# A convolution stage that keeps its outputs in other pieces, loads its bands once and shifts its seven-product blocks by one

## The chip, the core and the metric

One core of one Trainium2 chip runs the whole program in one launch. The metric is device time in microseconds; the kernel before was run three times, and its median stands for it. The five instruction streams are TensorE (PE, with its weight loads PEld), VectorE (DVE), ScalarE (ACT), GpSimd (POOL) and SyncE (SP), which here issues every DMA, in order.

## The reference

A decoder trunk with two layers on x of 1024 tokens by 1024 channels, all in float32. Only layer 0's token mixer is touched by the change:

```python
def conformer_conv(x, w_in, b_in, w_dw, b_dw, ln_g, ln_b, w_out, b_out):
    h = x @ w_in + b_in                       # 1024 -> 2048 channels
    a, gate = jnp.split(h, 2, axis=-1)
    h = a * jax.nn.sigmoid(gate)
    h = lax.conv_general_dilated(             # causal, 31 taps, each channel by itself
        h, w_dw[:, None, :], window_strides=(1,), padding=[(CONV_WIDTH - 1, 0)],
        dimension_numbers=("NWC", "WIO", "NWC"), feature_group_count=D_MODEL) + b_dw
    h = jax.nn.silu(layer_norm(h, ln_g, ln_b))
    return h @ w_out + b_out
```

After it come, in layer 0, a residual layer norm, a squared-ReLU MLP of 4096 channels, a second layer norm and a gated embedding; in layer 1 the same with sliding-window attention as mixer. They hold most of the time and keep their code.

## The kernel before

**Exact products in three passes.** A float32 operand is split into a high part (a cast on ACT) and a low part (a subtraction on DVE), and each product is three matmuls: high by high, high by low, low by high (`mm3`). The names show it: xh and xl hold the transposed activations in quarters by channel half and token half, wh and wl a weight unit of 128 x 1024, raw its load.

**The order is written by a program.** Every operation is first recorded; `schedule()` then plays the list through with a price for each operation and a free time for each engine, takes the ready operation of least rank, and so fixes the order in which each engine gets its instructions. Tiles are slots of a named pool (X 8, A 9, B 8, E 4, z 4, t 5, g 4), given out in the order of the recorded list; an operation that needs one waits until a slot is free. `later(n)` pushes the rank back by n, `after(op)` adds a dependence. SP is one line: a DMA that waits holds up all behind it. In `schedule()` a DMA was priced by its bytes alone:

```python
            if e == "sync":
                v = o.allv[0]
                dma = max(dma, t + 1400.0) + v.n * v.parts / 75.0
                finish(o, max(dma, t + 2800.0))
```

**The convolution stage, `conv()`**, is two generators stepped in turn, `taps` six steps (LAG) behind `conv_in`, each with four steps for one of eight blocks c of 128 channels.

- `conv_in(c)` makes the gated input of block c. Blocks 0 to ALONE - 1 do it in full: two token halves by two channel sets (gate and a) by eight k blocks by three, 96 matmuls of 512 columns. The others go through `conv_seven`: seven products of half the size on each side instead of eight, 84 matmuls, from sums and differences of the weights (`pair_units`) and of the activations, the forms T1 to T4. `forms()` makes T1 to T3 from fresh loads of xT, ranked 200 later, into places borrowed from the pools A, bo, v, B and X; T4 overwrites the activations' own tiles (channels 0 to 511 of the second token half) when block ALONE begins (`last_forms`), and two more E tiles become bands.
- `hand_over` splits the result g into a tile zz (wh for the very last) and writes it in eight DMAs to the DRAM tiles scr, from where `taps` reads it into B as G in another arrangement.
- `taps(c)` runs the depthwise convolution on TensorE: for each half jj of a block two groups j, two matrices k each, nine shifts, 36 matmuls of 256 columns. The stationary operand is a band, a 128 x 1152 tile E whose 64 left columns hold the high part of the taps on all 128 partitions and whose right ones hold, on partitions 0 to 63 (HIGH), the low part. It is made from a load z of w_dw with 128 x 576 values, in which the host had written the same 64 rows twice. ACT copies z into E, DVE subtracts.
- The sums are biased, transposed back to tokens (tr) and, for c < KEPT, copied into a t tile and written to the DRAM tile kept. From block KEPT on they are copied straight into the tiles Z (eight from pool X, eight from A). When block KEPT begins, sixteen DMAs bring the kept blocks into Z; a token row there lies in pieces of 64 values, 256 B.
- `conv_ln` then normalises each token row of Z on DVE and POOL, transposes it and applies SiLU; `mix_out` multiplies with w_out. The projection of the embedding (`embed(0, ...)`) is ranked 300 later and fills in between; its results and the bands of the last blocks share the time with all of that.

The call of `embed`, `conv_ln` and `mix_out`, the MLPs and the attention are the same before and after.

Of the kernel before, what the change touches and what calls it, by code (L numbers as in the profile page):

```python
# [10 lines left out]
F32 = mybir.dt.float32  # L11
F32R = mybir.dt.float32r
# [3 lines left out]
P = 128  # L16
# [32 lines left out]
             ps=6, tr=2, sc=0, pv=0, mid=0)  # L49


ALONE = 3
KEPT = 7
FORMS_BY, BACK_BY = 200, 300
FORM_HOMES = ("A", 9), ("bo", 2), ("v", 1), ("B", 4), ("X", 8)
LATE = 100
# [66 lines left out]
class View:  # L123
# [30 lines left out]

    def to_broadcast(self, shape):
        return View(self.buf, np.broadcast_to(self.idx, shape[1:]), self.parts, self.steps + (("bro", shape),))

    def real(self):
        a = self.buf.tile
# [37 lines left out]
class Recorder:  # L197
# [120 lines left out]
    def schedule(self):  # L318
# [85 lines left out]
        while True:  # L404
            best = None
            for e in engs:
                while rdy[e] and rdy[e][0][2].end:
                    heapq.heappop(rdy[e])
                while fut[e] and fut[e][0][3].end:
                    heapq.heappop(fut[e])  # L410
                if rdy[e]:
                    t = free[e]
                elif fut[e]:
                    t = max(free[e], fut[e][0][0])
                else:
                    continue
                if best is None or t < best[0]:
                    best = (t, e)
            if best is None:
                break  # L420
            t, e = best
            while fut[e] and fut[e][0][0] <= t:
                r, p, i, o = heapq.heappop(fut[e])
                if not o.end:
                    heapq.heappush(rdy[e], (p, i, o))
            p, i, o = heapq.heappop(rdy[e])
            if WAIT and fut[e] and e != "tensor":
                r, p2, i2, o2 = fut[e][0]
                if not o2.end and r <= t + WAIT and p2 < p - 300:
                    heapq.heappush(rdy[e], (p, i, o))  # L430
                    heapq.heappop(fut[e])
                    t, o = r, o2
            if o.eng == "either":
                o.eng = e
                o.dur = self.cost(o, o.outv, o.allv)
            d = o.dur
            if e == "scalar" and o.name == "activation":
                k = TABLE.get(o.args[2].name if len(o.args) > 2 else "", 0)
                if k and k != table:
                    table = k  # L440
                    d += 1283.0
            if both(o):
                d += max(0.0, held["gpsimd" if e == "vector" else "vector"] - 50.0 - t)
                held[e] = t + d
            free[e] = t + d
            if e == "sync":
                v = o.allv[0]
                dma = max(dma, t + 1400.0) + v.n * v.parts / 75.0
                finish(o, max(dma, t + 2800.0))
            else:  # L450
                finish(o, t + d)
# [47 lines left out]
class Emit:  # L499
# [318 lines left out]
    def conv(self):  # L818
# [8 lines left out]
        ws.add(*[lambda k=k: self.prep(d["w_in"][0, k], range(4 * k, 4 * k + 4)) for k in range(2)])  # L827
        ws.pump()
        for c in range(1, 8):
            ws.add(*([d["w_in"][c, 0], d["w_in"][c, 1]] if c < ALONE else self.pair_units([d["w_in2"][c - ALONE, k] for k in range(2)])))  # L830
        nc.sync.dma_start(cc, d["cconst"])
        nc.sync.dma_start(self.ident, d["ident"])
        scr = {}
# [1 line left out]

        def hand_over(c, h, g):

            both = self.sb("wh" if (c, h) == (7, 0) else "zz", F32R, 2 * HT)
            self.split(g, both[:, 0:HT], both[:, HT : 2 * HT])
            for j in range(NG):  # L840
                if j % 2 == 0 and (c, j // 2) not in scr:
                    scr[c, j // 2] = nc.tile(f"scr{c}_{j // 2}", (P, 2 * U), F32, "DRAM")
                o = j % 2 * U + h * P
                cols = slice(o, o + P)
                dst = scr[c, j // 2].scatter(
                    lambda a, cols=cols: a.rearrange("(k p) u -> p k u", p=CG)[:, :, cols], CG, cols, 2 * PH
                )
                src = both.bitcast(F32)[j * CG : (j + 1) * CG, :].rearrange("p (k u) -> p k u", k=2 * PH)
                nc.sync.dma_start(dst, src)
# [84 lines left out]

        def conv_in(c):

            if c >= ALONE:
                yield from conv_seven(c)
                return
            us = ws.get(2)  # L940
            for h in (0, 1) if c == 0 else (1, 0):
                pp = [self.ps() for s in range(2)]

                def part(s, kb):
                    wh, wl = us[kb // 4]
                    o = (kb % 4) * 256 + (1 - s) * P
                    tr = [(wh[:, o : o + P], wl[:, o : o + P], *self.xs(kb, h * HT, HT))]
                    self.mm3(pp[s], tr, kb == 0, kb == KB - 1)

                if c == 0:  # L950
                    for kb in range(KB):
                        part(0, kb)
                        part(1, kb)
                    yield
                else:
                    for s in range(2):
                        for kb in range(KB):
                            part(s, kb)
                        if s == 0:
                            yield  # L960
                sg = self.sb("t")
                nc.scalar.activation(sg, pp[0], AF.Sigmoid, bias=bg[:, c : c + 1], scale=1.0)
                g = self.sb("t")
                nc.vector.scalar_tensor_tensor(
                    out=g, in0=pp[1], scalar=ba[:, c : c + 1], in1=sg, op0=ALU.add, op1=ALU.mult
                )
                hand_over(c, h, g)
                yield
            ws.done(2)
# [3 lines left out]
        def taps(c):  # L973
# [3 lines left out]
            for jj in range(2):  # L977
                pss = [self.ps() for k in range(2)]
                for j in range(2):
# [3 lines left out]
                    nc.sync.dma_start(G2[:, :, HIST : HIST + U], scr[c, 2 * jj + j].rearrange("p (k u) -> p k u", k=2))  # L983
                    exchange = nc.ops[-1]
                    for k in range(2):
                        w = nc.tile("z", (P, n))
                        nc.sync.dma_start(w, d["w_dw"][c, jj, 2 * j + k])
                        w = w.rearrange("p (m q) -> p m q", q=PH * CG)
                        e = bands[turn[0] % len(bands)]
                        turn[0] += 1  # L990
                        ev = e.rearrange("p (m o q) -> p m o q", o=2, q=PH * CG)
                        if e in fresh:
                            fresh.remove(e)
                            nc.gpsimd.memset(ev.bitcast(F32)[LOW, :, 1, :], 0.0)
                        nc.scalar.copy(ev[:, :, 0, :], w)
                        nc.vector.tensor_tensor(
                            out=ev[HIGH, :, 1, :], in0=w[HIGH], in1=ev[HIGH, :, 0, :].bitcast(F32), op=ALU.subtract
                        )
                        for i in range(SHIFTS):
                            o = k * LO + HIST - i  # L1000
                            nc.tensor.matmul(
                                pss[k][:, j * U : (j + 1) * U], e[:, i * P : (i + 1) * P], G[:, o : o + U],
                                start=i == 0, stop=i == SHIFTS - 1,
                            )
# [19 lines left out]
                        nc.tensor.transpose(pv[:, h, j], y[:, o : o + P], self.ident)  # L1024
                nc.slack = 0.0
                if c < KEPT:
                    s = self.sb("t")
                    (nc.scalar.copy if jj else nc.vector.tensor_copy)(s, pt)
                    nc.sync.dma_start(kept[:, (2 * c + jj) * HT : (2 * c + jj + 1) * HT], s)
                    yield  # L1030
                    continue
                if c == KEPT and jj == 0:
                    kv = kept.rearrange("p (c s u) -> p c s u", c=2 * KEPT, s=2 * PH)
                    for q in range(2):
                        m = min(8, 2 * KEPT - 8 * q)
                        for h in range(2):
                            for f in range(PH):
                                Z[h, f, q] = self.sb("XA"[q])
                                dst = Z[h, f, q][:, 0 : 64 * m].rearrange("p (c u) -> p c u", u=64)
                                with nc.later(BACK_BY):  # L1040
                                    nc.sync.dma_start(dst, kv[:, 8 * q : 8 * q + m, PH * h + f, :])
                for h in range(2):
                    for f in range(PH):
                        o = c % 4 * P + jj * 4 * CG
# [43 lines left out]
            forms()  # L1088
        more_bands()
        kept = self.dram("kept", 2 * KEPT * HT)  # L1090
        ins = (x for c in range(8) for x in conv_in(c))
        outs = (x for c in range(8) for x in taps(c))
        for n in range(32 + LAG):
# [902 lines left out]
def layout(a):  # L1996
# [12 lines left out]
    r["xT"] = c(x[phased].T.reshape(KB, P, T))  # L2009
    r["pT"] = c(np.stack([p[0][phased], p[1]]).transpose(0, 2, 1).reshape(2, 2, P, T))  # L2010
    wi = np.asarray(a["conv_w_in"])[0]
    r["w_in"] = c(wi.reshape(2, 4, P, 2, 8, P).transpose(4, 0, 2, 1, 3, 5).reshape(8, 2, P, 1024)[:ALONE])

    w2 = wi[:, np.concatenate([np.arange(D, 2 * D), np.arange(D)])].reshape(8, P, 2, 8, P)
    r["w_in2"] = c(w2.transpose(3, 2, 1, 0, 4).reshape(8, 2, P, 1024)[ALONE:])
# [12 lines left out]
    for q in range(CG):  # L2028
        band[:, :, :, :, q, :, q] = wt[:, :, :, :, q, :]
    band = band.reshape(8, 2, 4, P // 2, SHIFTS * PH * CG)  # L2030
    r["w_dw"] = c(np.concatenate([band, band], axis=3))

    bd = np.asarray(a["conv_b_dw"])[0].reshape(32, 2, CG).transpose(2, 1, 0).reshape(CG, 64)
    r["cconst"] = c(
# [45 lines left out]
```

## Time and profile before

| | us |
|---|---|
| runs | 2140.18, 2142.8, 2143.06 |
| median | 2142.8 |
| profiled execution | 2142.3 |
| its span, first to last instruction | 2140.5 |
| TensorE busy | 2116.5 |
| VectorE busy | 1757.5 |
| ScalarE busy | 1152.3 |
| GpSimd busy | 280.6 |

The mean granted TensorE clock is 0.999. The DMA moved 462.46 MB, of 228,939 packets 38,192 under 512 B. Nearly every instruction carries one line, L466, where the recorded list is issued, so rows are told apart by the tiles that they write and read: `ps<-xh,wl` is a matmul into PSUM, `E<-z` the making of a band, `X<-kept` a read of kept outputs. A group's mean for a matmul counts its pipelined duration (389 ns), which overlaps the next; how many of them start in a stretch says more. A row of a timeline gives start, duration, engine, line, operation, tiles and how many were merged.

### The profile page before, as it was taken

How to read it: one execution, taken by the hardware profiler on the slowest of the kernel's cores; microseconds unless marked ns; L12 is line 12 of the kernel's file. 1: busy time of each engine (PE TensorE's matmuls, PEld its weight loads, DVE VectorE, ACT ScalarE, POOL GpSimd, SP SyncE). 2: the span in 40 equal slices, each digit the busy share in tenths (PEclk: the TensorE clock that was granted, in tenths of full speed). 3: DMA queues.
4: the chain of work that ended last, by engine and by line, in shares of the span. 5: the costliest groups of instructions: out<-in, count | busy, mean ns of one | idle time of the engine just before them, and what ended most of it. 6: DMA issues, size and time to landing. Idle time of an engine off the chain costs nothing.

```text
span 2140.5 us, 29992 instructions
## 1 busy us (share of the span) xinstructions
PE 2116.5 (99%) x10008; PEld 1752.9 (82%) x10008; DVE 1757.5 (82%) x2854; ACT 1152.3 (54%) x2146; POOL 280.6 (13%) x495
## 2 busy tenths in 40 slices
PE   9999899999999999999999999999999999999999
PEld 7888778888888888888788888888888888888877
DVE  6866579988898788876986888689988988788688
ACT  5655554654544633335755888445445554333484
POOL 0000052200000000001320656240000000000042
PEclk9999999999999999999999999999999999999999
DMA  9877965867786756655487022665778795565726
GB/s 295 234 203 203 268 245 177 285 222 250 264 271 231 278 177 204 201 184 213 156 284 249 11 89 79 208 239 184 257 267 296 262 332 174 179 233 170 262 75 230
DMA packets 228939, 462.46 MB, mean 216 GB/s; under 512 B 38192, under 2 KB 64432, under 8 KB 228784
## 3 DMA queue, kind: packets, MB, share of 16 engines
q1 hardware_dynamic: 228784, 460.54, 65.1%
q8 instruction: 79, 1.29, 0.2%
q14 instruction: 76, 0.62, 0.1%
HBM read 312.34 MB, written 148.11 MB: 215 GB/s over the span
## 4 chain that ended last, share of the span: by engine, by line
PE 40%; DVE 5%; ACT 3%; DMA 2%; issue 1%; POOL 1%; SPq 0%; POOLq 0%; DVEq 0%; ACTq 0%
PE ps L466 31%; PE tr L466 9%; DVE xl L466 1%; DMA t<-proj 1%; ACT z L466 1%; DVE t L466 1%; POOL sm L466 1%; DVE z L466 1%; DVE sm L466 0%; DVE A L466 0%; DVE B L466 0%; ACT xh L466 0%; DMA raw<-in_w_kv_dram 0%; ACT t L466 0%; DMA raw<-gate_t 0%
## 5 line engine op out<-in xcount | busy, mean ns | idle before, releaser
L466 PE MATMUL ps<-xh,xl 128*128 128x512 f32 x636 | 247.6, 389 | 0.0
L466 PE MATMUL ps<-xh 128*128 128x512 f32 x636 | 247.6, 389 | 0.0
L466 PE MATMUL ps<-xl,xh 128*128 128x512 f32 x636 | 247.6, 389 | 0.0
L466 ACT CAST wh<-raw 128x1024 fp32r<-128x1024 f32 (+2 forms) x156 | 143.4, 923 | 134.7 <-PE ps L466 84.0
L466 POOL TENSOR_SCALAR sm<-sm 128x1 f32<-128x1 f32 x72 | 28.3, 397 | 1364.0 <-DVE E L466 612.0
L466 PE MATMUL ps<-xl,wh 128*128 128x512 f32 x508 | 198.7, 392 | 0.0
L466 PE MATMUL ps<-xh,wl 128*128 128x512 f32 x508 | 198.3, 391 | 0.0
L466 PE MATMUL ps<-xh,wh 128*128 128x512 f32 x508 | 196.1, 392 | 0.9 <-ACT xh L466 0.9
L466 PE MATMUL ps<-wh,xh 128*128 128x512 f32 (+1 forms) x404 | 159.2, 395 | 1.7 <-ACT zz L466 0.9
L466 PE MATMUL ps<-wh,xl 128*128 128x512 f32 (+1 forms) x404 | 160.4, 397 | 0.0
L466 PE MATMUL ps<-wl,xh 128*128 128x512 f32 (+1 forms) x404 | 159.3, 394 | 0.0
L466 ACT CAST wh<-g 128x512 fp32r<-128x512 f32 x128 | 76.4, 620 | 153.8 <-PE ps L466 73.7
L466 ACT CAST xh<-wh 128x1024 fp32r<-128x1024 f32 x76 | 79.7, 1049 | 118.0 <-PE tr L466 90.4
L466 PEld LDWEIGHTS ps<-xl,xh 128*128 128x128 f32 x636 | 119.4, 188 | 24.9
L466 PEld LDWEIGHTS ps<-xh,xl 128*128 128x128 f32 x636 | 119.4, 188 | 24.7
L466 PEld LDWEIGHTS ps<-xh 128*128 128x128 f32 x636 | 119.5, 188 | 24.6
L466 DVE TENSOR_TENSOR wl<-raw,wh 128x1024 fp32r<-128x1024 f32 (+1 forms) x100 | 100.0, 1001 | 35.5 <-ACT wh L466 35.1
L466 DVE TENSOR_TENSOR xl<-wh,xh 128x1024 fp32r<-128x1024 f32 x76 | 92.8, 1221 | 25.6 <-ACT xh L466 25.6
L466 PEld LDWEIGHTS ps<-xh,wh 128*128 128x128 f32 x508 | 95.4, 188 | 22.5 <-ACT xh L466 1.6
L466 PEld LDWEIGHTS ps<-xh,wl 128*128 128x128 f32 x508 | 95.5, 188 | 19.5
L466 PEld LDWEIGHTS ps<-xl,wh 128*128 128x128 f32 x508 | 95.4, 188 | 19.5 <-DVE xl L466 1.3
L466 DVE TENSOR_TENSOR wl<-g,wh 128x512 fp32r<-128x512 f32 x128 | 84.6, 686 | 26.8 <-ACT wh L466 26.8
(447 smaller groups left out, 5620.0 us busy)
## 6 DMA issues: line engine op xcount, KB each, us to landing
wh<-hid SPq DMA_DIRECT2D x78, 512.0 KB, 4.1
raw<-in_w_up_dram SPq DMA_DIRECT2D x61, 512.0 KB, 4.3
wl<-in_w_down_dram SPq DMA_DIRECT2D x58, 512.0 KB, 4.8
hid<-zz SPq DMA_DIRECT2D x96, 256.0 KB, 4.0
z<-in_w_dw_dram SPq DMA_DIRECT2D x64, 288.0 KB, 4.0
hid<-t SPq DMA_DIRECT2D x70, 256.0 KB, 3.0
raw<-hid SPq DMA_DIRECT2D x30, 512.0 KB, 3.7
B<-scr SPq DMA_DIRECT2D x32, 256.0 KB, 4.5
```

Of the source, the lines that this page charges most:

```text
L466: getattr(getattr(nc, o.eng), o.name)(*a, **k)
```

## The change

- `View.transfer()` is new: it counts the contiguous pieces of a view and prices 12 ns for each and 0.0476 ns for each byte, over 16. `schedule()` takes the larger of the two sides of a DMA instead of bytes over 75.
- ALONE 3 becomes 2, and block LAST = 7 is done in full: blocks 2 to 6 go by seven products. Because T4 has overwritten a quarter of the activations, `conv_in(7)` loads four blocks of xT again (`load_xT`), takes the token halves in the order 0, 1 and, in half 1, the blocks k from 4 on first. The very last `hand_over` is now (7, 1).
- KEPT 7 becomes 6. For the kept blocks the transposed result is copied by token half, h = 0 on DVE and h = 1 on ACT, into a t tile that holds both halves jj of the block, and written in one DMA for each h, in pieces of 128 values (512 B), to a layout in which each token phase has its six blocks side by side. The sixteen reads then take whole rows: 512 values for blocks 0 to 3, 256 for blocks 4 and 5.
- w_dw is stored once, 64 x 576. z has 64 partitions, ACT copies it twice (rows HIGH, rows LOW), DVE subtracts as before.

```diff
-ALONE = 3
-KEPT = 7
+ALONE = 2
+LAST = 7
+KEPT = 6
...
+    def transfer(self):
+        i = self.idx.ravel()
+        pieces = self.parts * (1 + int((np.diff(i) != 1).sum()))
+        return (12.0 * pieces + 0.0476 * 4 * i.size * self.parts) / 16
...
-                v = o.allv[0]
-                dma = max(dma, t + 1400.0) + v.n * v.parts / 75.0
+                dma = max(dma, t + 1400.0) + max(v.transfer() for v in o.allv)
...
-            if c >= ALONE:
+            if ALONE <= c < LAST:
                 yield from conv_seven(c)
                 return
             us = ws.get(2)
-            for h in (0, 1) if c == 0 else (1, 0):
+            if c == LAST:
+                for kb in range(KB // 2):
+                    self.load_xT(1, kb)
+            for h in (0, 1) if c in (0, LAST) else (1, 0):
                 pp = [self.ps() for s in range(2)]
+                order = [(kb + KB // 2 * (h if c == LAST else 0)) % KB for kb in range(KB)]
...
-                        w = nc.tile("z", (P, n))
+                        w = nc.tile("z", (P // 2, n))
...
-                        nc.scalar.copy(ev[:, :, 0, :], w)
+                        for rows in (HIGH, LOW):
+                            nc.scalar.copy(ev[rows, :, 0, :], w)
                         nc.vector.tensor_tensor(
-                            out=ev[HIGH, :, 1, :], in0=w[HIGH], in1=ev[HIGH, :, 0, :].bitcast(F32), op=ALU.subtract
+                            out=ev[HIGH, :, 1, :], in0=w, in1=ev[HIGH, :, 0, :].bitcast(F32), op=ALU.subtract
                         )
...
                 if c < KEPT:
-                    s = self.sb("t")
-                    (nc.scalar.copy if jj else nc.vector.tensor_copy)(s, pt)
-                    nc.sync.dma_start(kept[:, (2 * c + jj) * HT : (2 * c + jj + 1) * HT], s)
+                    for h in range(2):
+                        if jj == 0:
+                            wait[h] = self.sb("t")
+                        v = wait[h].rearrange("p (f j u) -> p f j u", f=PH, j=2)
+                        src = pt[:, h * 256 : (h + 1) * 256].rearrange("p (f u) -> p f u", f=PH)
+                        (nc.scalar.copy if h else nc.vector.tensor_copy)(v[:, :, jj, :], src)
+                        if jj:
+                            dst = kept.rearrange("p (s c u) -> p s c u", s=2 * PH, c=KEPT)
+                            nc.sync.dma_start(dst[:, PH * h : PH * h + PH, c, :], wait[h].rearrange("p (f u) -> p f u", f=PH))
...
-                                dst = Z[h, f, q][:, 0 : 64 * m].rearrange("p (c u) -> p c u", u=64)
+                                o = ((PH * h + f) * KEPT + 4 * q) * P
                                 with nc.later(BACK_BY):
-                                    nc.sync.dma_start(dst, kv[:, 8 * q : 8 * q + m, PH * h + f, :])
+                                    nc.sync.dma_start(Z[h, f, q][:, 0 : P * m], kept[:, o : o + P * m])
...
-    r["w_dw"] = c(np.concatenate([band, band], axis=3))
+    r["w_dw"] = c(band)
```

More of the change, by code (lines that the diff above doesn't have):

```diff
@@ L829, in conv @@
         for c in range(1, 8):
-            ws.add(*([d["w_in"][c, 0], d["w_in"][c, 1]] if c < ALONE else self.pair_units([d["w_in2"][c - ALONE, k] for k in range(2)])))
+            ws.add(*([d["w_in"][c, 0], d["w_in"][c, 1]] if c < ALONE or c >= LAST else self.pair_units([d["w_in2"][c - ALONE, k] for k in range(2)])))
         nc.sync.dma_start(cc, d["cconst"])
@@ L836, in hand_over @@
         def hand_over(c, h, g):
-            both = self.sb("wh" if (c, h) == (7, 0) else "zz", F32R, 2 * HT)
+            both = self.sb("wh" if (c, h) == (LAST, 1) else "zz", F32R, 2 * HT)
             self.split(g, both[:, 0:HT], both[:, HT : 2 * HT])
@@ L947, in part @@
                     tr = [(wh[:, o : o + P], wl[:, o : o + P], *self.xs(kb, h * HT, HT))]
-                    self.mm3(pp[s], tr, kb == 0, kb == KB - 1)
+                    self.mm3(pp[s], tr, kb == order[0], kb == order[-1])
                 if c == 0:
@@ L956, in conv_in @@
                     for s in range(2):
-                        for kb in range(KB):
+                        for kb in order:
                             part(s, kb)
@@ L1032, in taps @@
                 if c == KEPT and jj == 0:
-                    kv = kept.rearrange("p (c s u) -> p c s u", c=2 * KEPT, s=2 * PH)
                     for q in range(2):
-                        m = min(8, 2 * KEPT - 8 * q)
+                        m = min(4, KEPT - 4 * q)
                         for h in range(2):
@@ L1090, in conv @@
         kept = self.dram("kept", 2 * KEPT * HT)
+        wait = {}
         ins = (x for c in range(8) for x in conv_in(c))
@@ L2011, in layout @@
     wi = np.asarray(a["conv_w_in"])[0]
-    r["w_in"] = c(wi.reshape(2, 4, P, 2, 8, P).transpose(4, 0, 2, 1, 3, 5).reshape(8, 2, P, 1024)[:ALONE])
+    r["w_in"] = c(wi.reshape(2, 4, P, 2, 8, P).transpose(4, 0, 2, 1, 3, 5).reshape(8, 2, P, 1024))
     w2 = wi[:, np.concatenate([np.arange(D, 2 * D), np.arange(D)])].reshape(8, P, 2, 8, P)
```

## The prediction, made before the changed kernel was run

> **What bounds the kernel now.** I read the page first, then busy time by stretch, then the waits, and last the order of time around the one place that stands out.
>
> ```profile
> span 2140.5 us, 29992 instructions
> PE 2116.5 (99%) x10008; PEld 1752.9 (82%) x10008; DVE 1757.5 (82%) x2854; ACT 1152.3 (54%) x2146; POOL 280.6 (13%) x495
> ```
>
> The kernel is bound by TensorE: 24.0 us of the span are without a matmul. The profiled run took 2142.3 us, 1.8 more than its span and 0.5 less than the median 2142.8, so I sum against 2142.3 and add 0.5 at the end. A change that leaves the matmuls alone can win only part of those 24.0 us and what a lower clock costs. The stretches tell where they lie (PE busy is the second figure, then its matmuls in brackets; PEclk, DMA share and GB/s end the row):
>
> ```profile
> core 0: us, PE busy (x) PEld busy (x) DVE busy (x) ACT busy (x) POOL busy (x), PEclk, DMA share, GB/s
> 100.00:150.00 50.00, 50.00 (x288) 43.85 (x288) 35.53 (x52) 29.98 (x54) 0.78 (x7) 1.00 0.69 204
> 200.00:250.00 50.00, 44.55 (x253) 38.32 (x252) 31.82 (x45) 27.44 (x48) 1.89 (x9) 0.97 0.92 244
> 250.00:300.00 50.00, 47.02 (x265) 39.12 (x264) 34.18 (x74) 30.66 (x62) 23.84 (x29) 1.00 1.00 336
> 850.00:900.00 50.00, 50.00 (x222) 41.43 (x221) 43.18 (x56) 18.09 (x23) 0.00 (x0) 1.00 0.71 235
> 1000.00:1050.00 50.00, 48.10 (x240) 38.87 (x240) 41.24 (x76) 40.05 (x78) 22.99 (x37) 1.00 0.12 36
> 1050.00:1100.00 50.00, 48.66 (x224) 39.91 (x223) 44.68 (x72) 30.18 (x48) 10.73 (x3) 1.00 0.80 282
> ```
>
> The MLP stretch (850) is full: 50 us / 222 = 0.225 us for a matmul of 512 columns. The end of the convolution is not: 5.45 us idle in 200:250 and 2.98 in 250:300, over a third of all idle time, and just there the DMA share is 0.92 and 1.00. That is where the kept outputs are read back. Who was waited for:
>
> ```profile
> PE ps L466 <- DVE E L466: 2.1, 2, 1.1
> PE ps L466 <- POOL X L466: 1.8, 1, 1.8
> PE ps L466 <- DVE g L466: 1.7, 2, 1.2
> PE ps L466 <- ACT xh L466: 1.6, 1, 1.6
> ```
>
> ```profile
> 225.00:230.00 5.00, 5.00 (x33) 4.49 (x32) 3.84 (x7) 2.82 (x4) 0.62 (x1) 1.00 1.17 229
> 235.00:240.00 5.00, 3.60 (x19) 2.99 (x17) 3.19 (x5) 3.21 (x7) 0.00 (x0) 0.69 0.94 299
> 240.00:245.00 5.00, 3.63 (x17) 2.74 (x18) 4.46 (x7) 3.49 (x7) 0.00 (x0) 0.97 0.89 221
> 285.00:290.00 5.00, 4.21 (x21) 2.95 (x21) 4.12 (x6) 2.58 (x6) 5.00 (x4) 1.00 1.05 402
> ```
>
> E are the bands of taps; behind "DVE E" stands a band that landed late (ScalarE's row of bands, below, waited 8.8 us for it). The granted clock fell to 0.69 for 5 us: 0.31 x 5 + 0.03 x 5 = 1.7 us lost beside the idle time. And a full queue moves 229 GB/s while kept pieces come in, 402 when rows are whole.
>
> **Matmuls.** Blocks 3 to 7 by seven products become blocks 2 to 6: five of eight as before, 84 matmuls instead of 96 each. Counted over the instruction lists, TensorE has the same number of each shape in both. Cost nothing; only order and waits are left.
>
> **DMA at the end of the convolution.**
>
> ```profile
> DMA packets 28212, 26.16 MB, mean 308 GB/s; under 512 B 16005, under 2 KB 19906, under 8 KB 28206
> z<-in_w_dw_dram SPq DMA_DIRECT2D x11, 288.0 KB, 4.5
> X<-kept SPq DMA_DIRECT2D x8, 256.0 KB, 6.2
> A<-kept SPq DMA_DIRECT2D x8, 192.0 KB, 5.3
> ```
>
> (DMA of 215:300.) The reads are 8 x 8 x 128 + 8 x 6 x 128 = 14,336 pieces of 256 B, nearly all of the small ones. After, they are 2 KB and 1 KB rows: 2.1 MB go from 229 to 402 GB/s (9.2 to 5.2 us), 1.57 MB become 1.05 (6.9 to 2.6): -8.3 us of queue time. Eleven half bands save 1.6 MB, -4.0 us; four reloads of 256 KB of xT for block 7 add 2.6. So some 9.7 of 85 us of queue go, and since the form tiles X and A come free a block earlier, all sixteen reads stand ahead of block 7's last writes in SP's line, instead of eight of them behind. I take the 5.45 us and the 1.7 of clock as gone: **-7.15**. Bounds: 0 and -7.15.
>
> What is next late is the exchange of block 7 itself (its products go to DRAM and come back as G for its taps), which needs no crowded queue to take time:
>
> ```profile
> 228.52 0.39 PE L466 MATMUL ps<-xh,wl 128*128 128x512 f32 x1
> 230.84 3.95 SPq L466 DMA_DIRECT2D kept<-t  x1
> 241.22 3.71 SPq L466 DMA_DIRECT2D scr<-wh  x8
> 246.89 1.89 SPq L466 DMA_DIRECT2D B<-scr  x3
> 252.07 8.77 PE L466 MATMUL ps<-B,E 128*128 128x256 f32 x72
> ```
>
> ```profile
> B<-scr SPq DMA_DIRECT2D x13, 256.0 KB, 3.8
> ```
>
> (The second is DMA of 100:200.) Before, 23.2 us pass from the block's last product to its first taps, SP standing 3.95 us at one kept write among them, and the list puts 54 taps, 35 matmuls and 8 transposes there: 54 x 8.77/72 + 35 x 0.225 + 0.9 = 15.4 us. After, 2 matmuls stay of the 35, 16 come among the last 72 taps and 17 behind them: 6.6 + 0.5 + 0.4 = 7.5. The chain by rows is about 2.9 (gating and low part on DVE at 0.68 each, a weight half of double width between them, 1.36, and 0.2 to pass on; the 0.68 is quoted under the start), 3.7 (eight writes issued), 0.6 (1.89/3, the read issued), 3.8 (landing) = 11.0. Exposed: **+3.5**. Bounds: 0, if the reads land faster, and 7.8, what was lost there before (23.2 - 15.4).
>
> This one wait is longer than the two of 1.1 us that preceded the 0.69, but the 1.8 us on POOL X left 1.00, so I take no clock loss; in the range, 1.7. By the Trainium skill (TensorE: Matmul & The Clock Gate, "Why this matters for your kernels") gaps over some 3 us drop the array to half rate; by it the sum would be 1.7 higher. The trace's drop after two short gaps doesn't agree with gap length as the only trigger.
>
> **Layer norm behind it.**
>
> ```profile
> 269.07 0.19 POOL L466 TENSOR_SCALAR sm<-sm 128x1 f32<-128x1 f32 x1 [41.61 <-DVE sm L466]
> ```
>
> It starts on POOL 8.2 us after the last taps (252.07 + 8.77), behind reads of A that SP still issued meanwhile. After, all of Z is there before, and the 17 matmuls put behind the taps cover 3.8 us more of the chain. Of 2.98 us I take **-1.7**; bounds 0 and -2.98.
>
> **The start.**
>
> ```profile
> 63.66 0.68 DVE L466 TENSOR_TENSOR X<-g,X 128x512 fp32r<-128x512 f32 x1
> 66.18 0.68 DVE L466 TENSOR_TENSOR X<-g,X 128x512 fp32r<-128x512 f32 x1
> 95.26 0.63 PE L466 MATMUL ps<-A,wh 128*128 128x512 f32 x2
> ```
>
> The forms T1 to T3 are complete at 66.9, but first used at 95.3: 28 us of room. After, 96 matmuls, 90 taps and 12 transposes fewer stand ahead: 21.6 + 11.0 + 1.2, so 95.3 - 33.8 = 61.5, and the last part of T2 (ready at 64.3) is read by its tenth product, 61.5 + 10 x 0.225 = 63.7. **+0.6**. A wait that isn't there before can't fall below nothing; the upper bound is a rival below. The reload of xT costs TensorE nothing while block 7's first half (5.4 us a product) covers it.
>
> **Bands on ScalarE.**
>
> ```profile
> L466 ACT CAST E<-z 128x576 fp32r<-128x576 f32 x64 | 42.6, 667 | 14.6 <-DMA z<-in_w_dw_dram 8.8 <-PE ps L466 3.0 <-PE tr L466 2.3
> L466 ACT ACTIVATE g<-ps,cst 64x256 f32<-64x256 f32 x64 | 28.1, 465 | 22.2 <-PE ps L466 21.7
> L466 DVE TENSOR_TENSOR E<-z,E 64x576 fp32r<-64x576 f32 x64 | 47.2, 746 | 39.4 <-ACT E L466 26.9 <-PE ps L466 12.3
> ```
>
> DVE takes 746 ns over 64 rows, no less than its 680 over 128 rows of 512, so I take a copy of half the rows at the full 667: 64 more, +42.7 us of ACT. In 100:150 that is 14 of them: 30.0 + 9.3 of 50 us, hidden. In the tail without products 36 taps (4.4 us) need eight copies and four activations, 7.2 us: 2.8 short twice, inside the exchange wait: 0, bounds 0 and 5.6. Kept outputs are now copied by halves on both engines, and two of the five t tiles are held until the second half; the kept write still stands in SP's line with scr writes and G reads queued behind it: 0, bounds -1 and +2.
>
> **The rest.** schedule() now prices each DMA by its pieces: by its own two formulas a whole 512 KB row load counts 5% less than before and 256 KB the same, so order shifts everywhere. Between 400 and 1000 there is hardly idle time to win; 1000 to 1100 has 3.2. I take 0, with 2.5 to either side.
>
> Sum: 2142.3 - 7.15 + 3.5 - 1.7 + 0.6 = 2137.5, with 0.5 for the median **2138.0 us**.
>
> **Rivals.** One, all waits go, exchange included: 2142.8 - 7.15 - 2.98 = 2132.7. For it: the list lets taps follow closely. Against: the chain of rows above. Two, half bands take as long as full ones, so the queue stays full where bands and reads meet: half of the 7.15 and 1.0 of the 1.7 stay: 2138.0 + 3.6 + 1.0 = 2142.6, no change. No row has a 64-row load; that kept pieces halve the rate speaks for pieces as the cause. The Trainium skill (SBUF — State Buffer, "Door 1: The DMA port swizzle") says that partitions 0 to 63 reach eight of sixteen ports, with the bandwidth of 32; no run here shows it yet. By that rule this rival happens. Three, slower: the forms are late. Block 2 needs its own weight sums now, while DVE makes the forms: four sums and five low parts at 0.68 and one of double width, 7.5 us; with four more band copies (2.7) and the clock (1.7) TensorE stands: 2138.0 + 11.9 = 2149.9. It decides from where T2's last part comes 4.8 us late, at 63.7 + 4.8 = 68.5; then the gain is spent. Against it: the list keeps most of these parts behind the forms.
>
> **How the numbers follow.** About 0.2%, 4.3 us, is what can be told from no change: faster is below 2138.5, slower above 2147.1. Forecast 0.56, with a range of its own of 2134 to 2142, split 0.33 faster and 0.23 same; rival one 0.13, faster; two 0.11, same; three 0.20, slower. So 0.46, 0.34, 0.20. The range leaves out rival three's share: from rival one with 1.2 of reordering below it, 2131.5, to 2147.0, which is rival two with 4.4 of the open bounds (ACT 5.6, clock 1.7, order 2.5).
>
> **What would show it.** DMA share in 225:300 below 0.9; the clock at 1.00 in 225:250; one wait of PE on taps of about 4 us near 235; PE idle in 200:300 of 4 to 6 instead of 8.4; the first products of T2 near 62 with under 1 us waited. Wrong would be PE waits on X or A from DVE between 60 and 75, half bands landing as late as full ones, or new idle time after 330.

## The result and the profile after

The changed kernel takes 2154.0 us (five runs, 2153.1 to 2160.1) against 2143.1 (five runs) before: ratio 1.0059, 95% interval 1.0042 to 1.0076, 11 us slower. The forecast was 2138.0, with a range up to 2147.0. The profiled execution is the slowest of the five, 2160.1 us, so its account is some 6 us larger than the median's. Its page:

```profile
span 2158.4 us, 30104 instructions
PE 2124.2 (98%) x10008; PEld 1758.0 (81%) x10008; DVE 1766.2 (82%) x2865; ACT 1197.4 (55%) x2227; POOL 290.4 (13%) x501
```

The span is 17.9 us longer: TensorE stands 34.2 us instead of 24.0, and the same 10008 matmuls take 7.7 us more. By stretch, first after and then before (columns as in the prediction):

```profile
60.00:125.00 65.00, 58.90 (x316) 49.56 (x315) 48.72 (x75) 48.77 (x87) 1.47 (x9) 0.95 0.60 163
200.00:245.00 45.00, 43.47 (x249) 37.69 (x248) 29.56 (x43) 30.68 (x53) 3.38 (x7) 1.00 0.95 247
245.00:330.00 85.00, 77.32 (x416) 65.33 (x415) 59.35 (x119) 53.85 (x109) 24.82 (x32) 0.96 0.63 208
1000.00:1375.00 375.00, 367.85 (x1899) 301.08 (x1898) 299.56 (x693) 273.07 (x755) 160.57 (x325) 1.00 0.43 146
```

```profile
60.00:125.00 65.00, 64.43 (x371) 56.11 (x370) 53.37 (x81) 42.30 (x77) 2.26 (x12) 1.00 0.76 218
200.00:245.00 45.00, 41.15 (x240) 35.82 (x239) 30.16 (x43) 24.82 (x44) 1.89 (x9) 0.96 0.92 241
245.00:330.00 85.00, 80.06 (x416) 65.85 (x415) 59.74 (x114) 42.81 (x82) 27.21 (x32) 1.00 0.75 243
1000.00:1375.00 375.00, 370.17 (x1916) 302.86 (x1916) 300.55 (x698) 273.87 (x759) 154.08 (x322) 1.00 0.42 144
```

60 to 125 stood 0.6 us and stands 6.1; 200 to 245 gains 2.3; 245 to 330 loses 2.7, and 1000 to 1375 2.3. ScalarE is busier in each of the first three. The waits of PE between 60 and 330 (total, times, longest):

```profile
PE ps L472 <- DMA B<-scr: 6.9, 3, 3.4
PE ps L472 <- ACT t L472: 2.1, 3, 1.7
PE tr L472 <- DVE g L472: 2.1, 2, 1.1
PE ps L472 <- DVE g L472: 2.1, 1, 2.1
PE tr L472 <- POOL X L472: 1.5, 1, 1.5
```

No band is waited for any more; G is, at 110.6 (3.1 us) and before block 7's taps. And the granted clock:

```profile
110.00:115.00 5.00, 4.45 (x19) 4.35 (x20) 1.43 (x2) 1.34 (x2) 0.00 (x0) 0.50 0.73 202
115.00:120.00 5.00, 5.00 (x23) 4.13 (x22) 1.34 (x3) 1.92 (x4) 0.11 (x1) 0.87 0.48 136
250.00:255.00 5.00, 0.73 (x2) 0.30 (x2) 2.54 (x6) 3.35 (x9) 0.00 (x0) 0.79 0.65 159
255.00:260.00 5.00, 4.33 (x20) 4.25 (x21) 1.73 (x4) 2.57 (x6) 0.00 (x0) 0.53 0.95 242
1260.00:1265.00 5.00, 5.00 (x23) 4.38 (x22) 4.33 (x13) 4.88 (x21) 2.15 (x6) 0.68 0.31 106
```

Summed over all rows of 5 us below 1.00, as (1 - clock) x 5 us and up to 2130, 8.5 us are lost to the clock (two smaller rows, 105 at 0.95 and 1255 at 0.98, belong to these) against 1.7 before. Idle (+10.2) and clock (+6.8) make up 17.0 of the 17.9.

### The profile page after: what moved, and what is told of

Its sections match the earlier page's. It is cut to its first block, busy times and chain, and to the rows that moved or that the text cites. A ratio compares the mean times of both kernels' runs of the same rounds, so it can differ in the third digit from the quotient of the medians.

```text
span 2158.4 us, 30104 instructions
## 1 busy us (share of the span) xinstructions
PE 2124.2 (98%) x10008; PEld 1758.0 (81%) x10008; DVE 1766.2 (82%) x2865; ACT 1197.4 (55%) x2227; POOL 290.4 (13%) x501
## 4 chain that ended last, share of the span: by engine, by line
PE 42%; ACT 3%; DVE 3%; DMA 2%; issue 1%; POOL 0%; SPq 0%; ACTq 0%; POOLq 0%; DVEq 0%
PE ps L472 30%; PE tr L472 13%; ACT z L472 1%; DVE t L472 1%; DMA t<-proj 1%; DVE B L472 0%; DMA raw<-in_w_kv_dram 0%; ACT t L472 0%; DMA down_low_t<-xl 0%; POOL sm L472 0%; ACT xh L472 0%; DMA raw<-in_w_q_dram 0%; DMA raw<-gate_t 0%; ACT wh L472 0%; DVE z L472 0%
## 5 line engine op out<-in xcount | busy, mean ns | idle before, releaser
L472 PE MATMUL ps<-xh 128*128 128x512 f32 x600 | 233.4, 389 | 0.0
L472 PE MATMUL ps<-xl,xh 128*128 128x512 f32 x600 | 233.4, 389 | 0.0
L472 PE MATMUL ps<-xh,xl 128*128 128x512 f32 x600 | 233.4, 389 | 0.0
L472 PE MATMUL ps<-wh,xh 128*128 128x512 f32 x380 | 151.5, 399 | 2.2 <-ACT zz L472 1.0
L472 PE MATMUL ps<-wl,xh 128*128 128x512 f32 x380 | 151.8, 399 | 0.2 <-DMA wl<-gate_low_t 0.2
L472 PE MATMUL ps<-wh,xl 128*128 128x512 f32 x380 | 151.1, 398 | 0.0
L472 PEld LDWEIGHTS ps<-xl,xh 128*128 128x128 f32 x600 | 112.6, 188 | 23.6
L472 PEld LDWEIGHTS ps<-xh 128*128 128x128 f32 x600 | 112.6, 188 | 23.3
L472 PEld LDWEIGHTS ps<-xh,xl 128*128 128x128 f32 x600 | 112.6, 188 | 23.3
```

The source lines that it names most:

```text
L472: getattr(getattr(nc, o.eng), o.name)(*a, **k)
```

## The experiments

Four theories: A, the shifted blocks cost the time; B, the new price spoils the order; C, the handling of kept outputs; D, the half bands with their second copy on ScalarE. A fifth, E, came after the first eight runs: that any new plan loses. Each part was taken out of the changed kernel (x) and put alone into the kernel before (y). Intervals are of 95%; the kernel before had medians of 2141.8 to 2143.4 beside them. Each of x1 to x4, y1 to y4, n1, b1, c3, d1 and d2 has a list planned anew; z1 to z3, c1 and c2 keep a given order. The diffs are shortened.

**x1: the old price in the changed kernel.**
```diff
-dma = max(dma, t + 1400.0) + max(v.transfer() for v in o.allv)
+dma = max(dma, t + 1400.0) + o.allv[0].n * o.allv[0].parts / 75.0
```


> The changed kernel (2154.0) with the old price of a DMA in the planner (bytes over 75); all else as changed. Theory A, the shifted blocks cost the time (the exchange of block 7 exposed by 5.5 us, the wait for G at 110 of 3.1 us, each with 3.4 us of clock): the two waits stay, 2150 to 2156. Theory B, the new price puts DMAs in an order in which G comes late: the wait at 110 and its clock go (-6.5) and perhaps the T1-before-T3 wait of 1.7 at 66, 2145 to 2148. Theories C (kept copies on ScalarE) and D (half bands): no change, 2152 to 2156.


2158.4 us, ratio 1.0080 (1.0066 to 1.0093): slower still, above every expectation. With this list the new price helps, if anything, by some 4 us (the two intervals overlap); B's version of it is out.

**x2: blocks 3 to 7 by seven products again.**
```diff
-ALONE = 2; LAST = 7; KEPT = 6
+ALONE = 3; LAST = 8; KEPT = 7
```


> The changed kernel with blocks 3 to 7 by seven products again and seven kept blocks (still in the new layout, rows of 512 and 384 values); half bands and new price stay. Theory A: the waits at 66, 110 and before block 7's taps go, with the clock lost there (2154 - 1.7 - 6.5 - 5.5 - 3.4 and + 2 to 4 for an exchange as before): 2137 to 2141. Theory B: the wait for G in the first blocks stays in some form, 2147 to 2152. C and D: 2150 or more.


2149.5, ratio 1.0033 (1.0023 to 1.0043): 4.5 us back, short of what A expected. (The very last hand_over is (7, 0) again.)

**x3: kept outputs as before (KEPT = 6).**
```diff
-wait[h] = self.sb("t"); halves of pt copied for both jj; 512 B written, rows read
+s = self.sb("t"); (nc.scalar.copy if jj else nc.vector.tensor_copy)(s, pt); 256 B read
```


> The changed kernel with the kept outputs copied and written as before (whole copies in turn on VectorE and ScalarE, pieces of 256 B read back), for six kept blocks. If the new layout is what I took it for, relief of the DMA queue at 225 to 300, time rises by 2 to 7 us to 2156 to 2161. Theory C, that the copies by halves on ScalarE delay the T products at 66 and hold t tiles: time falls by 1.7 to 4 us, 2150 to 2152. A, B, D: 2153 to 2156.


2150.3, ratio 1.0037 (1.0025 to 1.0050): 3.7 us back, as C had it. The wait for G at 110 is gone. The timelines show why; SP in the changed kernel, what ScalarE waited for in it, then SP in x3:

```profile
85.76 1.08 SPq L472 DMA_DIRECT2D kept<-t  x2
94.98 5.38 SPq L472 DMA_DIRECT2D scr<-zz  x8
103.52 3.66 SPq L472 DMA_DIRECT2D scr<-zz  x8
107.34 2.65 SPq L472 DMA_DIRECT2D B<-scr  x4
```
```profile
89.58 0.69 ACT L472 ACTIVATE t<-ps,cst 128x512 f32<-128x512 f32 x1 [0.39 <-DMA kept<-t]
```
```profile
85.90 3.79 SPq L472 DMA_DIRECT2D scr<-zz  x8
94.22 3.64 SPq L472 DMA_DIRECT2D scr<-zz  x8
98.45 1.01 SPq L472 DMA_DIRECT2D B<-scr  x1
```

The gated input of block 2 needs a t tile; with two of five held over both halves, it starts after a kept write has landed, and its products go to DRAM at 95.0 instead of 85.9.

**x4: whole bands again.**
```diff
-w = nc.tile("z", (P // 2, n)); for rows in (HIGH, LOW): nc.scalar.copy(ev[rows, :, 0, :], w)
+w = nc.tile("z", (P, n)); nc.scalar.copy(ev[:, :, 0, :], w)
```


> The changed kernel with the bands stored twice again (288 KB loads on 128 partitions, one copy on ScalarE instead of two). Theory D, the 64 added copies of 0.67 us on ScalarE and 128 waits cost the time: 2145 to 2149. Theory A or B: the same waits with a fuller queue, 2154 to 2159.


2145.1, ratio 1.0017 (1.0008 to 1.0026): 8.9 us of 11 come back, as D expected. The list is planned anew here too, so the 8.9 hold the copies and the order together.

**y1 to y4: each part alone in the kernel before.** The edits are the plus side of the change (y3 for seven kept blocks).


> The kernel before (2143.1) with only the new price of a DMA in the planner. Theory B (the price spoils the order): 2148 to 2154. Theory A: the order moves a little, 2141 to 2146.


2155.7, ratio 1.0065 (1.0052 to 1.0077). Nothing but order differs, and it loses 13.8 us, while x1 shows no loss by the same price. Its waits in 200 to 330:

```profile
PE ps L471 <- DVE xl L471: 4.2, 1, 4.2
PE ps L471 <- ACT t L471: 4.1, 2, 3.2
```

Both lie behind the convolution, at 276 and 306, in the layer norm and the product after it.

> The kernel before with only the blocks shifted: two ordinary blocks first, 2 to 6 by seven products, 7 in full, six kept blocks in the old layout. Theory A: 2150 to 2160, with a wait of several us for G before block 7's taps. Theory B: 2141 to 2146.


2146.8, ratio 1.0022 (1.0013 to 1.0031): 4.9 us, less than A expected, of which one wait for G before block 7's taps is 4.2.


> The kernel before with only the new handling of the kept outputs (copies by halves, 512 B written, rows of 512 and 384 values read; seven kept blocks). If the small pieces caused the idle 5.5 us and the 1.7 us of clock at 225 to 250: 2136 to 2139. If the bands that land late there have another cause (their place in the line of SP): 2142 to 2145.


2144.7, ratio 1.0013 (1.0004 to 1.0022): slower by 2.8. The first expectation, a gain from fewer small pieces, fails; the second, that the bands are late for another cause, holds.


> The kernel before with only the half bands (144 KB loads, two copies on ScalarE each). Theory D: 2147 to 2152. If the queue at 225 to 250 is the bound there and half bands relieve it: 2138 to 2142. If 64 partitions take as long as 128: 2142 to 2145.


2154.5, ratio 1.0058 (1.0046 to 1.0071): 12.6 us from the one part that I had costed at nothing. The four losses sum to 34, the change lost 11: the parts don't add.

**z1: half bands in the order of before; z2: the order planned for half bands, with whole ones.** The planner was given the one kernel's operations and the other's were issued in their places, so that every engine's order is held. Below is z1.
```diff
 nc.sync.dma_start(w, d["w_dw"][c, jj, 2 * j + k])
+nc.instead[nc.ops[-1]] = [("dma_start", (w[HIGH], d["w_dw"][c, jj, 2 * j + k]), {})]
...
 nc.scalar.copy(ev[:, :, 0, :], w)
+nc.instead[nc.ops[-1]] = [("copy", (ev[rows, :, 0, :], w[HIGH]), {}) for rows in (HIGH, LOW)]
```


> The kernel before with half bands loaded and copied twice, but every engine's instructions in the order of before: the planner still sees one load of 288 KB and one copy on ScalarE, and only what is issued differs (beside each copy stands its second half). Theory E, the half bands alone cost 12.6 us because the list was planned anew, not because of the loads or copies: 2139 to 2145. Theory D, the 64 added copies and their place ahead of other work on ScalarE cost it: 2148 to 2155.


2152.8, ratio 1.0049 (1.0037 to 1.0061). As D expected: with no new plan at all the half bands cost 10.8.


> The counterpart: the order planned for half bands, but whole bands loaded and copied once, as before. Theory E: 2150 to 2156, as the half bands in this order (2154.5). Theory D: 2141 to 2146.


2153.1, ratio 1.0053 (1.0041 to 1.0064). As E expected: the order planned for half bands loses as much (11.2) with whole ones. So the 12.6 of y4 are not the two losses added up; z1, not y4, tells what the half bands cost by themselves.

**z3: whole-row reads in the order of before.** Small pieces are moved from the reads to the writes.
```diff
-kept[:, (2 * c + jj) * HT : (2 * c + jj + 1) * HT]
+kept.rearrange("p (s c u) -> p s c u", c=2 * KEPT, s=2 * PH)[:, :, 2 * c + jj, :]
```


> The kernel before with the order of before on every engine; only the layout of the kept outputs in DRAM differs: each of the 14 writes goes in pieces of 256 B, and the reads at the end take whole rows of 2 KB and 1.5 KB. If the small pieces read there cause the two waits on late bands and the clock of 0.69 at 235 (4 to 7 us): 2135 to 2139. If the bands are late for their place in SP's line or the writes pay it back: 2141 to 2144.


2139.3, ratio 0.9991 (0.9983 to 1.0000): 2.7 us won by the medians, 3.6 at most by the interval; that lies between the two expectations.

**n1: a neutral new plan.**
```diff
-dma = max(dma, t + 1400.0) + v.n * v.parts / 75.0
+dma = max(dma, t + 1400.0) + v.n * v.parts / 76.0
```


> A neutral change of the plan: the kernel before with bytes over 76 instead of 75 in the planner's price of a DMA, nothing else. Theory E (the order of before is a well chosen one, and planning anew costs by itself): 2146 to 2156. Theories A to D (the parts of the change cost by what they add): 2140 to 2144.


2140.4, ratio 0.9995 (0.9987 to 1.0004). TensorE's list differs from that of before in many places, though in fewer than y1's, and nothing is lost: E fails as a rule. A new order can cost 14 us or nothing.

**c1: whole loads, two copies; c2: half loads (as in z1), second copy on GpSimd; both in the order of before.**
```diff
+nc.instead[nc.ops[-1]] = [("copy", (ev[rows, :, 0, :], w[rows]), {}) for rows in (HIGH, LOW)]   # c1
+[("scalar", "copy", (ev[HIGH, :, 0, :], w[HIGH]), {}), ("gpsimd", "tensor_copy", (ev[LOW, :, 0, :], w[HIGH]), {})]   # c2
```


> The kernel before, its order and its whole bands of 288 KB; only each copy of a band on ScalarE is issued as two of 64 rows. If the copies (0.67 us each, 64 more) cost what the half bands cost in this order (10.8 us): 2150 to 2154. If the loads do: 2141 to 2144.


2152.7, ratio 1.0045 (1.0031 to 1.0059).


> The kernel before in its order with half bands of 144 KB, where the second copy of 64 rows is GpSimd's and ScalarE makes one. If the copies on ScalarE are the cost and GpSimd's copy (0.7 to 1.5 us) hides: 2138 to 2143. If the half loads cost it: 2149 to 2154. If GpSimd's copy is slow or keeps VectorE from SBUF, so that bands come later: over 2146.


2143.1, ratio 1.0003 (0.9994 to 1.0012). For the order of before this settles it: the second copy on ScalarE is the price of the half bands, and the half loads neither cost nor win what this can tell. ScalarE in c1, and in the kernel before at the same place of the list:

```profile
91.30 0.47 ACT L468 ACTIVATE g<-ps,cst 64x256 f32<-64x256 f32 x1
91.67 4.14 ACT L468 CAST E<-z 64x576 fp32r<-64x576 f32 x6
95.83 0.83 ACT L468 ACTIVATE g<-ps,cst 64x256 f32<-64x256 f32 x2
```
```profile
87.07 0.47 ACT L466 ACTIVATE g<-ps,cst 64x256 f32<-64x256 f32 x1
87.44 0.66 ACT L466 CAST E<-z 128x576 fp32r<-128x576 f32 x1
89.42 1.41 ACT L466 CAST E<-z 128x576 fp32r<-128x576 f32 x2 [1.32 <-DMA z<-in_w_dw_dram]
90.86 0.83 ACT L466 ACTIVATE g<-ps,cst 64x256 f32<-64x256 f32 x2
```
```profile
PE tr L468 <- DVE g L468: 3.9, 2, 2.7
```

Six copies, where three stood before, are ahead of the activations that free the tap sums; VectorE's g and the transposes on TensorE follow them, and TensorE waits (the last row, PE in 60 to 125 of c1; the 2.7 are at 97.4). ScalarE is busy 42.3 of the 65 us from 60 to 125 before and 51.4 in c1: far from full, and yet late. This is not all: of the 10.5 us by which c1's span is longer, 4.7 are idle time in 60 to 125, 3.4 are lost clock, and 2.4 are one wait of TensorE at 1747, in layer 1, where there is no band. z1, z2 and y4 wait there too (1.6 to 2.8 us), the kernel before and c2 don't; why stays open.

**c3: the changed kernel with the second copy on GpSimd.**
```diff
-for rows in (HIGH, LOW): nc.scalar.copy(ev[rows, :, 0, :], w)
+nc.scalar.copy(ev[HIGH, :, 0, :], w); nc.gpsimd.tensor_copy(ev[LOW, :, 0, :], w)
```


> The changed kernel with the second copy of a band on GpSimd, the plan made with it. If the copies on ScalarE are most of the change's loss: 2144 to 2149, the waits for G at 110 and 256 shorter. If not: 2152 to 2158.


2150.8, ratio 1.0035 (1.0023 to 1.0048): 3.2 back, between the two expectations. Waits for G of 2.7 at 111 and 4.3 at 254 stay. A copy on GpSimd takes 0.86 us here against 0.67 on ScalarE; whether later bands or the new order kept the rest isn't shown.

**b1: z3's layout with n1's plan.**


> A version that may beat both: whole-row reads of the kept outputs (2139.3 in the order of before) in the order planned with bytes over 76 (2140.4). If their gains add: 2136 to 2139. If both end at the same waits at 235 to 250: 2139 to 2141.


2139.9, ratio 0.9986 (0.9977 to 0.9994): faster than both kernels, and no better than z3 alone.

**d1: shifted blocks and kept outputs only (whole bands, old price); d2: x4 with the forms not put back.**


> The changed kernel without half bands and without the new price: only the shifted blocks and the kept outputs in larger pieces. With half bands taken out alone it was 2145.1. If the shift itself costs at the start (7 us more at 60 to 125) and gains at the end (10 us less at 200 to 330): 2141 to 2146. If the price helps this list, as it did with half bands (2158.4 without it, 2154.0 with it): 2147 to 2151.


2146.9, ratio 1.0018 (1.0010 to 1.0027), within 2 us of x4.
```diff
-FORMS_BY, BACK_BY = 200, 300
+FORMS_BY, BACK_BY = 0, 300
```


> The changed kernel with whole bands (2145.1) and the forms T1 to T4 not ranked 200 later but in the place where they are recorded. If the loss at 60 to 125 is work that crowds before block 2 (forms, weight sums and bands on VectorE and ScalarE): the first products of T2 wait less, 2140 to 2144. If it is the weight sums and G alone: 2144 to 2150, since the forms then push the bands back.


2142.1, ratio 0.9995 (0.9986 to 1.0005): no slower than before. What is late at the start is in part the forms' crowd, 2.0 of its 5.9 us of idle time. x4 and d2:

```profile
60.00:125.00 65.00, 59.06 (x325) 50.49 (x324) 52.38 (x81) 41.02 (x75) 1.47 (x9) 0.97 0.72 211
200.00:330.00 130.00, 128.32 (x701) 109.11 (x700) 97.33 (x172) 71.05 (x139) 30.40 (x38) 1.00 0.75 250
```
```profile
60.00:125.00 65.00, 61.01 (x343) 53.19 (x342) 50.78 (x78) 38.68 (x71) 1.58 (x10) 0.97 0.77 220
```

With whole bands the end of the convolution stands 1.7 us of 130 (before 3.85 + 4.94), but the start 5.9 (before 0.6). In d2 a wait for G of 3.2 at 108 is left.

## Why the prediction was wrong

**Bands on ScalarE: the step that failed.** The duration was right: the 64-row copy takes 671 ns, as the 128-row one did (667), and ScalarE got 42 us more of such copies. The reading of it failed: I averaged it over a stretch ("30.0 + 9.3 of 50 us, hidden") and priced it at 0, at most 5.6. With the order held the half bands cost 10.8 (z1), the two copies with whole loads 9.9 (c1), and nothing once the second copy was GpSimd's (c2). The room was there by the sum (35% of 60 to 125), but c1's rows show the copies in line ahead of the activations that TensorE's next transposes wait for. How the 11 us of the changed kernel split between copies and order stays open: x4 gave 8.9 back and c3 only 3.2, both planned anew; z2 and y1 show that order alone can cost as much, and no run held the changed kernel's own order.

**DMA at the end: term -7.15.** Most signs that I named came: the share in 225:300 fell from 1.00 to 0.88, the clock in 225:250 rose to 1.00, no band was late. But the idle time in 200:300 was 7.7, not 4 to 6. Where the second copy is left out (x4) 200:330 wins 7.1 us of idle time and 1.7 of clock. The rates were read rightly: in z3, with the order held, the stretch that moved 229 GB/s moved 393, and 26.2 MB of 215:300 took 90.8% of the queue instead of 99.9%, 7.7 us less.

```profile
225.00:230.00 5.00, 5.00 (x33) 4.51 (x32) 5.00 (x9) 2.78 (x6) 1.60 (x1) 1.00 1.06 393
```

The time that a read takes from issue to landing did not fall; it counts what stands ahead in the queue too. The first row is z3, the next two the changed kernel, and before X took 6.2:

```profile
X<-kept SPq DMA_DIRECT2D x8, 256.0 KB, 6.9
```
```profile
X<-kept SPq DMA_DIRECT2D x8, 256.0 KB, 6.4
A<-kept SPq DMA_DIRECT2D x8, 128.0 KB, 3.0
```

What failed is the step from the queue to TensorE. ScalarE's waits for the loads of bands fell from 8.8 to 4.8 us in z3, yet TensorE's two waits for bands only from 2.1 to 1.9, the clock lost 1.7 as before, and the whole gain was 2.7. I had taken "DVE E" for a band that landed late. z3's rows show the first of the two waits behind something else:

```profile
229.88 0.68 ACT L466 CAST E<-z 128x576 fp32r<-128x576 f32 x1
232.36 0.69 DVE L466 TENSOR_TENSOR t<-t,t 128x512 f32<-128x512 f32 x1
232.97 0.74 DVE L466 TENSOR_TENSOR E<-z,E 64x576 fp32r<-64x576 f32 x1
233.76 1.33 PE L466 MATMUL ps<-B,E 128*128 128x256 f32 x9 [1.28 <-DVE E L466]
```

The band was loaded and copied by 230.6; its subtraction stood in VectorE's line behind the gating of the last block. In the kernel before, too, the copy was done at 232.9 and VectorE, busy without a gap from 229.2, came to it at 233.5; only the second wait ended on a load. It is the failed step once more: a place in line, not a share.

**The exchange of block 7: term +3.5**, measured 2.1 + 3.4 idle, and 3.4 of clock. The mechanism was right; the rows of TensorE and of SP:

```profile
242.16 6.81 PE L472 MATMUL ps<-B,E 128*128 128x256 f32 x54
251.50 0.50 PE L472 MATMUL ps<-wh,wh 128*128 128x512 f32 x1 [2.09 <-DVE g L472]
255.67 0.58 PE L472 MATMUL ps<-B,E 128*128 128x256 f32 x1 [3.44 <-DMA B<-scr]
```
```profile
241.96 3.83 SPq L472 DMA_DIRECT2D A<-kept  x8
245.91 5.14 SPq L472 DMA_DIRECT2D scr<-wh  x8
251.16 0.48 SPq L472 DMA_DIRECT2D z<-in_w_dw_dram  x1
251.75 0.56 SPq L472 DMA_DIRECT2D B<-scr  x1
```

From the last product (242.2) to the first taps 13.5 us passed, not 11.0: the writes started 0.9 later than I had them, behind the reads of A, went out in 5.1 us instead of 3.7, and 0.7 passed at a band's load. The cover was 8.0, near what I had (7.5). But the term belongs to an order, not to the shift: with whole bands TensorE waited 0 (x4, d2), 2.8 (d1) or 4.2 us (y2) there.

**The start: term +0.6**, measured +5.5 idle and 3.4 of clock. The first products of T2 ran at 60.9 (I said 61.5) and waited 0.2, so rival three's condition, T2 after 68.5, did not come. Lost were 1.7 at 66, where the T1 products stood behind ScalarE's read of the T2 sums, 1.1 at 94 and 3.1 on G at 110, in a stretch that I had not looked at beyond T2. Its largest wait comes from **the t tiles held**, which I bounded at +2: every kernel here with both the shift and the new copies (the changed one, x1, x4, c3, d1, d2) waits 2.5 to 3.2 us at one place between 107 and 115; those with the shift alone (x3, y2) or the copies alone (x2, y3) don't. That the gate of block 2 stood behind a kept write is shown by ScalarE's row; that all six waits come from there is inferred.

**The layer norm: -1.7**, about right: TensorE waits 1.8 us for X from GpSimd, where it waited 3.3 for X and A. **The rest: 0 with 2.5 to either side** was too narrow. 1000:1375 lost 2.3, and y1 shows that a price alone can cost 14 us by order; n1, that a new order can cost nothing. Why the price hurts one list and not the other stays open.

**Half loads as long as full (rival two)**: not quite. z1 and c1 differ in the loads alone:

```profile
60.00:125.00 65.00, 60.67 (x335) 51.93 (x334) 47.92 (x73) 51.88 (x90) 2.17 (x11) 0.97 0.60 159
60.00:125.00 65.00, 59.78 (x328) 51.24 (x328) 47.83 (x72) 51.38 (x88) 2.15 (x11) 0.97 0.69 199
```

40 GB/s less in 65 us is 2.6 MB less, for 0.09 x 65 = 5.9 us of the queue: here the bytes saved went at 440 GB/s, as if 64 rows took half of what 128 take. Over 0 to 300, with all 64 loads, 9.3 MB less save 10.8 us (77.5% against 81.1%), half as much for each byte. And from issue to landing a half load takes 3.7 us, a whole one 3.9. So a half load takes less of the queue than a whole one; between half of it and all of it the runs don't settle. By the Trainium skill (SBUF — State Buffer, "Door 1: The DMA port swizzle") 64 rows reach half of the ports, and half the bytes would take as long; the landing times here nearly agree, the queue's time doesn't. For the result it made no difference: c2, with half loads, is as fast as the kernel before.

## What to carry to other kernels

Before a second instruction on an engine off the critical path is called hidden, look at what stands behind it in that engine's line and when the critical engine needs that, not at the engine's busy share. A tile held longer is a wait for whoever needs the next tile of the pool; trace the chain from it to the matmul. Where a program writes the order, hold the order while testing what an edit costs, and change the order alone by a neutral amount: both were needed here to tell 10 us of copies from 14 us of order.

## What the runs showed of the hardware

A copy on ScalarE of 64 rows takes as long as one of 128 (671 and 667 ns); on GpSimd one of 64 rows takes 863 (c3) to 981 (c2). Reads in rows of 2 KB instead of pieces of 256 B raised what the full queue moved in 225 to 230 from 229 to 393 GB/s (z3). The clock is lost in equal steps: 1.7 us in the kernel before, five times that in the changed one, 1.7 in x2, x3, x4 and d2, 8.5 in y1, none in n1. The Trainium skill (TensorE: Matmul & The Clock Gate, "What's actually happening") tells of a free-running window of 3.4 us and of half rate after an idle one; one window at half rate would lose 1.7, an estimate from that page, and the traces agree. That page's idle window of as long, by which the prediction had its sum 1.7 higher, fits the waits of 3.1 and 3.4 us here; but 1.9 at 1259 was enough too, while 1.7 at 66 and one of 2.4 in n1 (in 200 to 330) were not.
